# Handing the tokens of a hybrid block over channel by row, with the RMS norm factor applied as a row

## The chip, the cores and the metric

The kernel runs on one core of a Trainium2 chip. The metric is device microseconds of one execution, as the median of several runs. A core has a matrix engine (TensorE, PE in the profile, with its weight loads as PEld), a vector engine (VectorE, DVE), a scalar engine (ScalarE, ACT), GpSimd (POOL) and SyncE (SP), from whose queue most transfers (DMA) are issued. SBUF is the on-chip memory of 128 partitions; PSUM holds the results of TensorE in eight banks of 128 x 512 floats. Each engine takes its instructions in the order in which they were written and waits on semaphores for the others.

## What is computed

Two layers over 256 latent tokens `x` and 256 context tokens `ctx`, 2048 channels each. The change touches only the start of the first layer: the RMS norm of both token sets and their modulation.

```python
def rms_norm(x, g):
    y = xf * lax.rsqrt(jnp.mean(xf * xf, axis=-1, keepdims=True) + EPS)
    return (y * g.astype(jnp.float32)).astype(x.dtype)

def modulate(h, shift, scale):
    return h * (1 + scale) + shift
...
        shift, scale, gate = adaln(c, ada_w[i], ada_b[i])
        h = modulate(rms_norm(x, norm_g[i]), shift[:, None], scale[:, None])
        if needs_ctx:
            shift_c, scale_c, gate_c = adaln(c_ctx, ada_w[i], ada_b[i])
            hc = modulate(rms_norm(ctx, norm_g[i]), shift_c, scale_c)
...
    p = h @ w_in
    pc = hc @ w_in[:, base:]
```

`adaln` multiplies silu(c) by the modulation weights `ada_w` (2048 x 6144), whose first two thirds are the shift and the scale. After this the first layer runs neighbourhood attention and a state-space scan in parallel, and the second layer a gated short convolution. All data are float32.

## The kernel before

**Products.** An f32 product is made of three products in a faster form: both sides are split into a high part in that form (fp32r) and a low part, the rest. `hH[kb]` and `hL[kb]` are the high and low part of the modulated tokens for channel block kb (16 blocks of 128 channels), with the channels on partitions and 512 columns of tokens: latent tokens 0 to 255, then context tokens 256 to 511. Weight tiles arrive in `raw` buffers of 128 x 1024; ACT casts the high part (L420, or in halves L440) and DVE subtracts it for the low part (L427, L443), in one of three places `w`.

**Start.** The first part of the kernel goes in eight groups j of two channel blocks. For each group come the eight blocks of modulation weights (`ada`, four for the scale A0, four for the shift S0), multiplied with the conditioning vectors (L719), turned by TensorE and summed (L732 to L738). Then the modulated tokens of the group's two blocks are made (L757 to L763), and the group's part of the products is run: K and V for four token tiles t (0 and 1 latent, 2 and 3 context), Q for the latent tiles, and the first state-space columns (B) for all. K and V partial sums are copied out of PSUM in group 0 and added up on DVE afterwards (L787, L789). In group 0 the code writes the products of the latent tiles first (L875 to L889), then waits for the context tiles (L890).

**The tokens.** `x` and `cx` come as rows: 128 tokens on partitions, 2048 channels along. `x_norm` squares each row in four pieces with a running sum, on ACT (L601) and DVE (L603), makes the factor (mean, plus epsilon, power -0.5 on POOL, L571 and L572) and multiplies the row by it in place (L613, L615). `x_pair` then turns the row by TensorE, 128 x 128 at a time (`turn`, L199), two channel blocks to a bank, and ACT and DVE copy the bank into `xnT` (L628, L629). For group 0 the context tiles are handled one after the other, and the rest of their transposes come later. The context rows lie in the same places as the latent rows (`KT`, `KL`), so their loads wait until the latent rows have been turned.

**Order.** What is written out next is decided by a planner (`Plan`, L38) that keeps an estimated time for each engine and for the DMA. Tasks are generators: each names the engine and the operands that it needs next, and `pump` (L278) writes a step of the first task in the list `urgent` (then `side`, `back`) whose operands are estimated to be ready in time; `force` (L299) writes the earliest possible step until a condition holds. The list starts with the latent tokens, then the modulation task `ada_gen`, then the context tokens (L843 to L845). `ada_gen` is one task: it takes the groups one after another, and within a group first the modulation, then the scaled tokens. Loads are taken from a queue, `loads`, by `issue` (L365), in the order in which they were appended (L529 to L543); each needs a free `raw` buffer, of which there are nine at the start. Weights that are ahead get split by `split` and `low_part` (L405, L424); the latent step of group 0 writes the splits of V and Q itself, right behind its scaled tokens (L767 to L770).

## Time and profile before

| | us |
|---|---|
| Median of 3 runs | 1760.9 |
| Lowest and highest run | 1760.85, 1765.14 |
| Profiled execution, its own time | 1760.31 |
| Span of the profiled execution | 1758.5 |
| First modulation product | 10.82 |
| First K product of group 0 | 23.35 |
| First K product of group 1 | 54.30 |

A line of a group view names the source line, the engine, the operation, the tiles (out<-in), the shapes and the count, and then the busy time, the mean time of one in ns, and the idle time of the engine just ahead with what ended it. A line of the timeline begins with the start and the length in us. PE lines are listed by the helper that records them: L195 for all products, L199 for all transposes. For products in the form 128 x 512 the printed duration of one (about 390 ns) overlaps with the next; the distance between starts is what counts.

### The profile page before, as it was taken

What the parts mean: (1) busy time and instruction counts of PE and PEld (TensorE: products, weight loads), DVE (VectorE), ACT (ScalarE), POOL (GpSimd) and SP (SyncE); (2) the same over time, 40 slices, a digit from 0 to 9 for tenths busy, and PEclk for the clock granted to TensorE, in tenths of its full rate; (3) what the DMA queues carried; (4) which work ended last, traced back from release to release, by engine and by line L of the source; (5) the groups of instructions that cost most, each with busy time, mean ns of one, the idle gap of its engine ahead of it and who ended that gap; (6) DMA issues with size and microseconds to landing.
All of it is one profiled execution on the core that took longest, in us unless ns stands there. A gap on an engine that the chain in (4) does not pass through costs nothing.

```text
span 1758.5 us, 25025 instructions
## 1 busy us (share of the span) xinstructions
PE 1736.7 (99%) x9451; PEld 1463.1 (83%) x9451; DVE 1223.6 (70%) x1978; ACT 773.4 (44%) x1330; POOL 31.6 (2%) x28
## 2 busy tenths in 40 slices
PE   6999999999999999999999999999999999999998
PEld 4777988889888889888888898888888888888887
DVE  5666887878685878686877787787668555555554
ACT  5333544445242436343435343564446444444442
POOL 0000100001000000000000000000000000000000
PEclk9999999999999999999999999999999999999999
DMA  9987644686756767656776557768767666666563
GB/s 362 342 307 258 209 143 138 183 246 191 234 165 195 219 205 227 210 175 210 220 213 193 166 185 255 246 221 284 274 222 228 195 188 192 192 191 188 190 208 121
DMA packets 202536, 377.66 MB, mean 215 GB/s; under 512 B 32384, under 2 KB 69040, under 8 KB 202416
## 3 DMA queue, kind: packets, MB, share of 16 engines
q1 hardware_dynamic: 195152, 369.49, 65.5%
q10 hardware_dynamic: 7264, 6.58, 1.1%
q8 instruction: 74, 1.21, 0.3%
q14 instruction: 46, 0.38, 0.1%
HBM read 370.62 MB, written 6.71 MB: 215 GB/s over the span
## 4 chain that ended last, share of the span: by engine, by line
PE 94%; DMA 2%; DVE 2%; issue 1%; ACT 0%; POOL 0%; SPq 0%; ACTq 0%; DVEq 0%; POOLq 0%
PE bank L195 91%; PE bank L199 3%; DMA tmp<-dram_csr 1%; DVE w L427 1%; DMA raw<-in_ada 0%; DMA tmp<-dram_exr 0%; DMA raw<-in_adaT 0%; DVE tmp L1235 0%; ACT w L420 0%; POOL statk L572 0%; DVE mix L1562 0%; SPq L583 0%; DVE raw L823 0%; DVE tmp L603 0%; DVE Vt L1012 0%
## 5 line engine op out<-in xcount | busy, mean ns | idle before, releaser
L420 ACT CAST w<-raw 128x1024 fp32r<-128x1024 f32 x343 | 359.5, 1049 | 530.4 <-PE bank L195 447.7
L427 DVE TENSOR_TENSOR w<-raw,w 128x1024 fp32r<-128x1024 f32 x343 | 416.6, 1217 | 231.4 <-ACT w L420 230.1
L195 PE MATMUL bank<-hH,w 128*128 128x256 f32 (+1 forms) x2064 | 488.0, 324 | 1.2 <-DVE w L427 1.1
L195 PE MATMUL bank<-w,hH 128*128 128x512 f32 x1280 | 407.4, 396 | 2.7 <-ACT hH L757 2.5
L195 PEld LDWEIGHTS bank<-hH,w 128*128 128x128 f32 x2064 | 344.7, 188 | 34.2 <-DVE w L427 2.1
L195 PE MATMUL bank<-hL,w 128*128 128x256 f32 (+1 forms) x1040 | 334.3, 321 | 0.0
L195 PEld LDWEIGHTS bank<-w,hH 128*128 128x128 f32 x1280 | 237.7, 189 | 54.4 <-issue 4.0
L195 PE MATMUL bank<-w,hL 128*128 128x512 f32 x640 | 249.9, 391 | 0.1
L195 PEld LDWEIGHTS bank<-hL,w 128*128 128x128 f32 x1040 | 196.3, 189 | 14.9
L195 PE MATMUL bank<-w,h 128*128 128x512 f32 x768 | 179.7, 390 | 0.0
L823 DVE CUSTOM_DVE_ANT_0 raw<-raw,csb 128x1024 f32<-128x1024 f32 x128 | 155.4, 1219 | 26.2 <-DMA raw<-in_adaT 24.0
L195 PEld LDWEIGHTS bank<-w,h 128*128 128x128 f32 x768 | 143.6, 188 | 29.6
L195 PEld LDWEIGHTS bank<-w,hL 128*128 128x128 f32 x640 | 120.5, 188 | 25.4 <-DVE hL L763 0.6
L195 PE MATMUL bank<-w,mix 128*128 128x512 f32 x588 | 138.3, 391 | 0.9 <-DVE w L427 0.9
L195 PEld LDWEIGHTS bank<-w,mix 128*128 128x128 f32 x588 | 109.5, 188 | 24.0 <-DVE w L427 1.3
L1235 DVE SCALAR_TENSOR_TENSOR tmp<-bank,cwh,tmp 128x508 f32<-128x508 f32 (+1 forms) x96 | 71.0, 744 | 1.8
L195 PE MATMUL bank<-KL,h 128*128 128x512 f32 x264 | 63.8, 389 | 0.0
L427 DVE TENSOR_TENSOR KL<-raw,KL 128x1024 fp32r<-128x1024 f32 x32 | 39.1, 1223 | 33.1 <-ACT KL L420 33.1
L427 DVE TENSOR_TENSOR wL<-raw,wH 128x1024 fp32r<-128x1024 f32 x31 | 37.9, 1224 | 33.5 <-ACT wH L420 33.4
L427 DVE TENSOR_TENSOR QL<-raw,QT 128x1024 fp32r<-128x1024 f32 x32 | 39.2, 1224 | 29.8 <-ACT QT L420 29.8
L195 PEld LDWEIGHTS bank<-KL,h 128*128 128x128 f32 x264 | 49.5, 188 | 10.2
L195 PE MATMUL bank<-QT,h 128*128 128x512 f32 x168 | 56.2, 391 | 0.0
(291 smaller groups left out, 1984.7 us busy)
## 6 DMA issues: line engine op xcount, KB each, us to landing
raw<-in_w_in SPq DMA_DIRECT2D x196, 512.0 KB, 3.9
raw<-in_adaT SPq DMA_DIRECT2D x128, 512.0 KB, 4.8
raw<-in_sc_in SPq DMA_DIRECT2D x128, 512.0 KB, 3.8
raw<-in_w_out SPq DMA_DIRECT2D x64, 512.0 KB, 5.0
raw<-in_ada SPq DMA_DIRECT2D x34, 512.0 KB, 6.9
raw<-in_sc_out SPq DMA_DIRECT2D x32, 512.0 KB, 4.1
PT<-in_ada SPq DMA_DIRECT2D x16, 512.0 KB, 6.9
raw<-in_w SPq DMA_DIRECT2D x16, 512.0 KB, 6.1
```

The lines of the kernel that those rows point to most:

```text
L195: E(T.matmul(o, l, r, start=start, stop=stop, skip_group_check=True))
L199: E(T.transpose(o, i, ident if k == 128 else ident[:k, :k]))
L420: E(S.copy(H, v))
L427: E(V.tensor_tensor(out=Lo, in0=v, in1=H.bitcast(F32), op=ALU.subtract))
L823: E(V.tensor_tensor_reduce(out=raw, in0=raw, in1=csb, scale=1.0, scalar=0.0, op0=ALU.mult, op1=ALU.add, accum_out=gp[:, h, m:m + 1]))
L1235: E(V.scalar_tensor_tensor(out=do, in0=di, scalar=cwh[:, 32 * k + ch:32 * k + ch + 1], in1=do, op0=ALU.mult, op1=ALU.add))
```

## The change

The host hands both token sets over with channels on partitions: `xt` in two tiles of 8 channel blocks x 256 tokens, `ct` as one array of 16 blocks x 256 tokens. The row norm, its in-place scaling, the transposes and the copies (`x_norm`, `x_pair`) go. A new task `squares` squares the tokens two blocks at a time and sums over channels on TensorE: each 128 x 128 piece of the squares is the stationary side, and a column of ones is the moving side, so that the sum of each token lands on its own partition. For the latent tokens each of the eight pieces goes to TensorE (4 products each, the squares on ACT and DVE in turn); for the context ACT squares all eight, DVE adds the first seven up, and the sum and the last piece go to TensorE. The factor is made on 128 x 2 as before, broadcast along the free axis and turned by TensorE, so that `Rb` holds it as a row, the same on every partition. The scaled tokens are then made from the plain ones: DVE multiplies by A0 and by the row, ACT adds S0 for the high part, DVE adds S0 and subtracts the high part for the low one. In group 0 the two context tiles are now made together.

The context goes into places of its own (`QT`, `QL` and four of the `hL` tiles), and its load stands between the weights V and Q of group 0. The late halves of the small tables and of the constants are loaded after group 3 instead of before the second group's modulation weights. In group 0 the modulation products wait for one block each, not for two.

```diff
-    w_seg(0, CK, CV, CQ)
-    loads.append(lambda: x_load(2))
-    loads.append(lambda: x_load(3))
-    loads.append(lambda: E(DMA.dma_start(sm[:, NFIRST:], small[:, NFIRST:])))
-    loads.append(lambda: E(DMA.dma_start(cs_[:, CFIRST:], const[:, CFIRST:])))
+    w_seg(0, CK, CV)
+    loads.append(lambda: c_load())
+    w_seg(0, CQ)
...
+        if j == 3:
+            loads.append(lambda: E(DMA.dma_start(sm[:, NFIRST:], small[:, NFIRST:])))
+            loads.append(lambda: E(DMA.dma_start(cs_[:, CFIRST:], const[:, CFIRST:])))
...
+    one, Rb, *lplace = [st([128, 512], ("Bl", "Cl")[kb] if kb < 2 else f"hL{kb}", name=f"p{kb}") for kb in range(KB)]
+    E(V.memset(one, 1.0))
+    cplace += lplace[10:]
+    xT = [[xrow[k // 8][:, (k % 8) * 256:(k % 8) * 256 + 256], None] for k in range(KB)]
...
+    def squares(c):
+
+        yield when(lambda: xT[15][c] is not None)
+        acc, ps = None, None
+        for k in range(0, KB, 2):
+            src = xrow[k // 8][:, (k % 8) * 256:(k % 8) * 256 + 512]
+            if c:
+                src = cplace[k // 4][:, (k % 4) * 256:(k % 4) * 256 + 512] if k < 8 else cplace[k // 2 - 2]
+            onact = k % 4 == 0 or c == 1
+            yield W_("ACT" if onact else "DVE", src)
+            sq = tmp()
+            if onact:
+                E(S.activation(sq, src, AF.Square))
             else:
+                E(V.tensor_tensor(out=sq, in0=src, in1=src, op=ALU.mult))
+            if c and k < KB - 2:
+                if k == 0:
+                    acc = sq
+                    continue
+                yield W_("DVE", sq)
+                E(V.tensor_tensor(out=acc, in0=acc, in1=sq, op=ALU.add))
+                give(free_t, sq)
+                continue
+            parts = [acc, sq] if c else [sq]
+            for p in parts:
+                yield W_("PE", p, nb=0 if ps is not None else 1)
...
+                for h in range(2):
+                    for t in range(2):
+                        mm(ps[:, t:t + 1], p[:, h * 256 + t * 128:h * 256 + (t + 1) * 128], one[:, :1], f and not (h or t), True)
+                give(free_t, p)
+        r = rx[:, 2 * c:2 * c + 2]
+        yield W_("DVE", ps)
+        E(V.tensor_scalar(out=r, in0=ps[:, :2], scalar1=1.0 / D, scalar2=EPS, op0=ALU.mult, op1=ALU.add))
+        E(G.tensor_tensor(out=r, in0=r, in1=mhalf[:, :2], op=ALU.pow))
+        yield W_("PE", r)
+        for t in range(2):
+            turn(ps[:, 256 + t * 128:256 + (t + 1) * 128], r[:, t:t + 1].to_broadcast([128, 128]))
         yield W_("ACT", ps)
+        E(S.copy(Rb[:, c * 256:(c + 1) * 256], ps[:, 256:]))
         give(free_b, ps)
+        got.add(("r", c))
...
-                    w_ = 2 if j == 0 else 4
+                    w_ = 1 if j == 0 else 4
...
-            for ts in ((0, 1), (2,), (3,)) if j == 0 else ((0, 1, 2, 3),):
-                yield when(lambda: all(("xm", t, j) in got for t in ts))
+            for cs in ((0,), (1,)) if j == 0 else ((0, 1),):
+                yield when(lambda: all(("r", c) in got for c in cs))
...
-                        E(S.activation(hH[kb][:, ok_], xnT[kb][:, ok_], AF.Identity, scale=A0[:, kb, k:k + 1],
-                                       bias=S0[:, kb, k:k + 1]))
-                        E(V.tensor_scalar(out=hf[:, ok_], in0=xnT[kb][:, ok_], scalar1=A0[:, kb, k:k + 1],
-                                          scalar2=S0[:, kb, k:k + 1], op0=ALU.mult, op1=ALU.add))
+                    for c in cs:
+                        oc = slice(256 * c, 256 * c + 256)
+                        E(V.scalar_tensor_tensor(out=hf[:, oc], in0=xT[kb][c], scalar=A0[:, kb, c:c + 1], in1=Rb[:, oc],
+                                                 op0=ALU.mult, op1=ALU.mult))
+                        E(S.activation(hH[kb][:, oc], hf[:, oc], AF.Identity, scale=1.0, bias=S0[:, kb, c:c + 1]))
...
-                    E(V.tensor_tensor(out=hL[kb][:, o], in0=hf[:, o], in1=hH[kb][:, o].bitcast(F32), op=ALU.subtract))
+                    for c in cs:
+                        oc = slice(256 * c, 256 * c + 256)
+                        E(V.scalar_tensor_tensor(out=hL[kb][:, oc], in0=hf[:, oc], scalar=S0[:, kb, c:c + 1],
+                                                 in1=hH[kb][:, oc].bitcast(F32), op0=ALU.add, op1=ALU.subtract))
...
-    spawn(urgent, x_gen(0), 1)
+    spawn(urgent, squares(0), 1)
     spawn(urgent, ada_gen(), 2, 1)
-    spawn(urgent, x_gen(1), 1)
+    spawn(urgent, squares(1), 2)
```

More of the change, by code (lines that the diff above doesn't have):

```diff
@@ L141, with kernel @@
 @with_exitstack
-def kernel(ctx: ExitStack, tc, x, cx, ada0, w0, adaT, w_in, w_out, sc_in, sc_out, rpb, small, const,
+def kernel(ctx: ExitStack, tc, x, xt, ct, ada0, w0, adaT, w_in, w_out, sc_in, sc_out, rpb, small, const,
                        strict, rows, out):
@@ L617, in x_pair, with c_load @@
-    def x_pair(k2, ts):
-        yield W_("PE", *[XS[4 * t + k2 // 2] for t in ts], nb=1)
-        ps = bank()
-        n = 128 * len(ts)
-        for k in range(2):
-            kb = 2 * k2 + k
-            for i, t in enumerate(ts):
-                turn(ps[:, k * n + i * 128:k * n + (i + 1) * 128], XS[4 * t + kb // 4][:, (kb % 4) * 128:(kb % 4) * 128 + 128])
+    def c_load():
+        n = 0
+        for p in cplace:
+            m = p.shape[1] // 256
+            E(DMA.dma_start(p, ct[:, n * 256:(n + m) * 256]))
+            for k in range(m):
+                xT[n + k][1] = p[:, k * 256:(k + 1) * 256]
+            n += m
@@ L739, in ada_gen @@
                 give(free_b, ps)
-            for ts in ((0, 1), (2,), (3,)) if j == 0 else ((0, 1, 2, 3),):
-                yield when(lambda: all(("xm", t, j) in got for t in ts))
-                spans = [(k, slice(max(256 * k, 128 * ts[0]), min(256 * k + 256, 128 * ts[-1] + 128)))
-                         for k in range(2) if {2 * k, 2 * k + 1} & set(ts)]
-                o = slice(128 * ts[0], 128 * ts[-1] + 128)
+            for cs in ((0,), (1,)) if j == 0 else ((0, 1),):
+                yield when(lambda: all(("r", c) in got for c in cs))
+                o = slice(256 * cs[0], 256 * cs[-1] + 256)
                 for kb in (2 * j, 2 * j + 1):
@@ L1989 @@
     force(lambda: not urgent, (urgent,))
-_INS = ['x', 'cx', 'ada0', 'w0', 'adaT', 'w_in', 'w_out', 'sc_in', 'sc_out', 'rpb', 'small', 'const', 'strict', 'rows']
+_INS = ['x', 'xt', 'ct', 'ada0', 'w0', 'adaT', 'w_in', 'w_out', 'sc_in', 'sc_out', 'rpb', 'small', 'const', 'strict', 'rows']
 def kernel(**inputs):
```

73 lines of the change are left out of this document (20 added, 53 removed).

## The prediction, made before the changed kernel had run

> **What bounds the kernel now.** I read the page first, then the windows of the first 75 us, then the engine timelines inside them. Times are in us from the start of the span.
>
> ```profile
> PE 1736.7 (99%) x9451; PEld 1463.1 (83%) x9451; DVE 1223.6 (70%) x1978; ACT 773.4 (44%) x1330; POOL 31.6 (2%) x28
> ...
> PE   6999999999999999999999999999999999999998
> ```
>
> TensorE is busy 1736.7 of 1758.5 us; only the first of the 40 slices (44 us each) is far from full. All idle time of TensorE is 21.8 us. The change touches the head of the kernel and the scaled rows that feed it, so it can gain idle time of the head, or TensorE work that is in the way there, and nothing more.
>
> ```profile
> 0.00:13.00 13.00, 2.06 (x16) 0.43 (x16) 6.00 (x22) 6.38 (x14) 1.31 (x6) 1.00 0.83 310
> 13.00:17.50 4.50, 4.50 (x40) 4.28 (x40) 2.65 (x7) 3.04 (x9) 0.00 (x0) 1.00 1.02 411
> 17.50:23.35 5.85, 3.75 (x54) 1.67 (x46) 2.02 (x9) 2.22 (x6) 0.00 (x0) 1.00 1.04 412
> 23.35:33.40 10.05, 10.05 (x37) 7.81 (x38) 7.23 (x16) 7.55 (x14) 0.55 (x1) 0.83 1.03 400
> ...
> 54.30:75.50 21.20, 21.20 (x143) 16.10 (x143) 12.76 (x23) 6.31 (x10) 0.00 (x0) 1.00 0.95 347
> ```
>
> The columns are the stretch, its length, the busy time of PE, PEld, DVE, ACT and POOL, the granted clock, the DMA share and GB/s. Up to 23.35, when the first K product starts, the DMA is full and TensorE is not: this part waits for data. From 54.30 on TensorE has no gap at all, and VectorE is busy 60% of the time. What lies between is the ground of this change:
>
> ```profile
> 33.40:54.30 20.90, 19.15 (x170) 13.09 (x168) 14.40 (x39) 13.81 (x32) 1.06 (x3) 1.00 0.91 361
> 33.40:54.30 20.90, 4.74 (x36) 3.81 (x35) 1.00 0.91 361
> ```
>
> The first row is the whole stretch, the second the transposes (L199) in it. So 20.90 - 19.15 = 1.75 us are idle there, and a transpose costs 4.74 / 36 = 0.132 us of TensorE.
>
> **Part one: the latent tokens, up to the first product.** The 32 transposes of x between 13 and 17.5 go, with the copies of L628 and L629. In their place come 8 squares of 512 columns on ACT and DVE (the row norm needed as many) and 32 f32 products with one moving column. The kernel already has such products elsewhere:
>
> ```profile
> L195 PE MATMUL bank<-const,half 128*128 128x1 f32 x32 | 4.0, 229 | 0.0
> L199 PE MATMUL bank<-const,x 128*128 128x128 f32 x64 | 8.8, 290 | 0.3 <-ACT x L613 0.3
> L195 PE MATMUL bank<-PT,cpad 128*32 128x256 f32 x128 | 8.6, 381 | 0.0
> ```
>
> By the code those 32 instructions are 16 products (an f32 product shows as two instructions, as do the products with cpad: 8 for the 4 of one block). So one product is 2 x 4.0 / 32 = 0.25 us against 0.132 for a transpose, and 32 of them are 8.0 us where 4.2 stood. [...]
>
> These 8.0 us start when the first half row of x is squared, near 6, and end near 14.5. The modulation blocks wait behind them, and their four blocks of the scale part then run at once. What sets the end of this part is data, not TensorE:
>
> ```profile
> 9.42 0.33 SPq L381 DMA_DIRECT2D xtm<-in_ada  x1
> 10.71 0.33 SPq L381 DMA_DIRECT2D yi<-in_w  x1
> ...
> xtm<-in_ada SPq DMA_DIRECT2D x1, 512.0 KB, 10.2
> ...
> 20.57 0.61 PE L195 MATMUL bank<-xtm,cpad 128*32 128x256 f32 x8
> ...
> 22.44 0.16 DVE L738 TENSOR_TENSOR S<-S,small 128x4 f32<-128x4 f32 x1
> 22.64 0.41 DVE L759 TENSOR_SCALAR tmp<-xm,A,S 128x256 f32<-128x256 f32 x1
> ```
>
> The last modulation block lands at 9.42 + 10.2 = 19.6 and its products run at 20.57, behind the others. Taken block by block (the width 1 of the change) they can start at about 20.0, so the shift is ready some 0.5 us earlier. Against that, the scaled row now goes DVE, then ACT, then DVE, while before ACT read the normalised row beside DVE: 0.41 us more ahead of the first product. I take zero, with -0.4 to +0.7 as ends (the second block of channels waits once more for DVE).
>
> **Part two: the context tokens.** Their load is put between the weights V and Q. Before, V and Q came first and the context rows behind them:
>
> ```profile
> 17.37 1.77 SPq L583 DMA_DIRECT2D x<-in_cx  x4
> ...
> DMA to landing us min/median/max: 4.1/7.9/11.0
> ...
> 32.94 0.39 PE L195 MATMUL bank<-w,hL 128*128 128x512 f32 x1
> 33.17 0.39 PE L195 MATMUL bank<-w,hH 128*128 128x512 f32 x1
> 33.40 0.38 PE L199 MATMUL bank<-const,x 128*128 128x128 f32 x2
> 35.13 0.50 PE L195 MATMUL bank<-w,hH 128*128 128x512 f32 x1 [1.36 <-ACT hH L757]
> ```
>
> The last context load was issued about 18.7 and landed about 29.7 (11.0, the longest). The bytes ahead of Q in the new order are the same as those ahead of this load, so **Q lands near 29.7** and the context near 28.5. Q's split is queued on ACT and DVE before the context's squares: the split is written out right behind the first scaled row, and by the planner's own clock the context is not due by then. From here I step along, with these durations:
>
> ```profile
> L420 ACT CAST w<-raw 128x1024 fp32r<-128x1024 f32 x343 | 359.5, 1049 | 530.4 <-PE bank L195 447.7
> L427 DVE TENSOR_TENSOR w<-raw,w 128x1024 fp32r<-128x1024 f32 x343 | 416.6, 1217 | 231.4 <-ACT w L420 230.1
> L601 ACT ACTIVATE tmp<-x 128x512 f32<-128x512 f32 x8 | 5.0, 622 | 0.9 <-DMA x<-in_x 0.4 <-DMA x<-in_cx 0.4
> L789 DVE TENSOR_TENSOR sz<-sz,bank 128x512 f32<-128x512 f32 x2 | 1.4, 688 | 0.8 <-PE bank L195 0.7
> L572 POOL TENSOR_TENSOR rx<-rx,const 128x1 f32<-128x1 f32 x4 | 2.2, 552 | 35.4 <-DVE rx L571 35.4
> ```
>
> Cast to 30.7, low part to 31.9; the third product of Q needs it, and ten more at 0.23 (the starts 32.94 and 33.17 above) end at 34.2: **0.8 later** than the 33.4 of before. ACT squares all eight pieces of the context behind the cast, to 30.7 + 8 x 0.52 = 34.9 (0.62 each, 0.1 overlapped). DVE adds the first seven in six steps of about 0.62, 31.9 to 35.6. TensorE, in order, stands before the column sums from 34.2 to 35.6: **1.4 idle**. The sums are 8 products, 8 x 0.25 = **2.0**, with the last landing near 37.8; scaling, power on POOL (0.55) and their hand-overs take until 38.7: **1.0 idle**. Two transposes of the broadcast factor are **0.26**. ACT copies the row, DVE and ACT make the first scaled block by about 40.5; TensorE meanwhile runs the scale part of the next modulation block, 32 instructions at 8.6 / 128 = 0.067, 2.1 us. That cover rests on the order: it has landed (nothing but small loads was ahead of it) and the task issues it right behind the scaled rows. Without it another 1.4 us are idle.
>
> The removed side of the same stretch: 32 transposes, 4.2, and the 1.75 idle, which were the waits for each context tile in turn. Sum: -4.2 - 1.75 + 0.8 + 1.4 + 2.0 + 1.0 + 0.26 = **-0.5 us**.
>
> **Part three: the other seven groups.** Each block of 128 channels has on DVE 0.73 for two operations (L759) and 0.69 (L763 of 512 columns) before, and four two-input operations of 256 columns after:
>
> ```profile
> 46.47 0.73 DVE L759 TENSOR_SCALAR tmp<-xm,A,S 128x256 f32<-128x256 f32 x2
> 47.60 0.69 DVE L763 TENSOR_TENSOR hL<-tmp,hH 128x512 fp32r<-128x512 f32 x1 [0.39 <-ACT hH L757]
> ...
> 23.33 0.43 DVE L763 TENSOR_TENSOR hL<-tmp,hH 128x256 fp32r<-128x256 f32 x1 [0.28 <-ACT hH L757]
> ```
>
> 1.42 becomes 4 x 0.40 = 1.6 to 1.7, so 0.5 us more in a group of 21.2 us in which DVE is idle 8.4. Nothing here waits for it as long as the rows are made a group ahead; I take zero. The late half of the small tables moves behind group 3, 0.4 MB or 1 us of DMA out of the head, which TensorE does not wait for: zero. Where the rows stay longer in their places, the next writer is the first K norm after all eight groups: zero.
>
> The profiled execution took 1760.3 (span 1758.5 and 1.8 around it), 0.6 under the median of 1760.9. Forecast: 1760.3 - 0.5 = **1759.8**, no change that could be told. About 0.3%, 5.3 us, is what a measurement of this kernel can tell from none.
>
> **Rivals.** *A second slow stretch of the clock.* Now there is one:
>
> ```profile
> 24.00:25.00 1.00, 1.00 (x5) 0.60 (x4) 0.90 (x3) 1.00 (x2) 0.00 (x0) 0.82 0.98 393
> 25.00:26.00 1.00, 1.00 (x4) 0.81 (x3) 1.00 (x3) 1.00 (x2) 0.00 (x0) 0.50 1.05 418
> ...
> 28.00:29.00 1.00, 1.00 (x6) 0.83 (x5) 1.00 (x4) 0.92 (x2) 0.00 (x0) 0.97 1.05 384
> ```
>
> It follows the thin stretch from 17.5 to 23.35 (TensorE busy 3.75 of 5.85), lasts about 3.4 us at 0.50 and so costs 1.7. The new wait from 34.2 to 38.7 holds only 2 us of one-column products. If that brings a second slow stretch, the time is 1759.8 + 1.7 = 1761.5. For it: the wait is as thin. Against: from 33.40 to 35.13 TensorE did next to nothing and the clock stayed at 1.00. Chance 0.25. [...]
>
> *The waits do not come.* If the context is squared before Q's split, the sums lie behind V's products and neither wait shows: 1.4 + 1.0 + 0.8 come off, 1756.6; if the slow stretch then falls where TensorE waits for data, 1.7 more, 1754.9. For it: the context lands before Q. Against: ACT and DVE keep their order, and Q's split was queued first. Chance 0.15, half of it under 1755.6; a start at the early end of its bound adds 0.03.
>
> *Slower: the longer chain in the groups.* Each block now goes DVE, ACT, DVE on 256 columns, and hH waits for the first DVE step. DVE also releases the product banks (the additions of L789, 0.69 each). Where it stands in order before ACT while a bank waits, TensorE loses the step ahead of ACT, 0.43, and the 0.28 by which DVE's four operations are longer: 0.7 a block, in 14 blocks 9.9 us, 1759.8 + 9.9 = 1769.7. It decides from the point at which only one bank is free when a block's rows are made; at half of the blocks it gives 1764.8. Against it: TensorE has no gap from 54.30 to 75.50 with the like waits now. Chance 0.15, two thirds of it over 5.3 us; waits of the head wider than my bounds add 0.03.
>
> *The change gives less than it says.* The transposes go, but the column sums put 80 instructions (10 us by the row) where 64 (8.8) were. That is inside the forecast.
>
> **How the numbers follow.** Forecast 0.45, slow clock 0.25, no waits 0.15, chain 0.15. The ends: price of the 16 instructions from 0.066 to 0.23 each, -1.0 to +1.7; the missing cover, +1.4; the start, -0.4 to +0.7. Range 1755.0 to 1765.5. Faster by over 0.3%: 0.11; slower: 0.13; the rest, 0.76, is within.
>
> **What would show it.** Right: the products with one moving column at 0.125 an instruction; Q's products ending 33.5 to 34.5; the column sums of the context starting 1 to 2 us later on DVE's add; the same point of the weights' order (first K product of group 1) within 1.5 us of 54.3, allowing for 1.9 us of the modulation of group 2 that stood ahead of it; no gap of TensorE afterwards. Wrong: the context's squares ahead of Q's cast on ACT; a clock of 0.50 again near 38 to 42; idle time of TensorE after 54 that names the scaled rows or the bank additions.

## The result and the profile after

| | before | after |
|---|---|---|
| Median of 7 runs each, side by side (us) | 1763.17 | 1773.84 |
| Lowest and highest | 1760.85, 1768.93 | 1770.47, 1778.70 |
| Ratio, 95% interval | | 1.0061 [1.0041, 1.0081] |
| Profiled execution, its own time | 1760.31 | 1778.70 |
| First K product of group 0 | 23.35 | 30.77 |
| First B product of group 0 (the group's last part) | 49.37 | 55.83 |
| First B product of group 1 | 70.60 | 79.75 |
| First B product of group 7 | 192.41 | 202.08 |

The change made the kernel slower by 10.7 us; forecast were 1759.8 and a range up to 1765.5. The profiled execution of the changed kernel is the slowest of its seven, 4.9 above their median, so below I count at milestones inside the head: at the first B product of group 7, the last of the groups, it stands at +9.67, which is nearly the whole difference of the medians. Source lines of the changed kernel are numbered on their own (L196 the products, L200 the transposes).

The first row is from the page of the changed kernel (busy time of the engines), the others are from its windows, cut at the milestones:

```profile
PE 1750.4 (99%) x9471; PEld 1472.7 (83%) x9471; DVE 1218.5 (69%) x1952; ACT 761.7 (43%) x1301; POOL 31.7 (2%) x26
```

```profile
13.00:17.50 4.50, 4.50 (x23) 4.50 (x22) 0.00 (x0) 0.00 (x0) 0.00 (x0) 1.00 1.02 411
17.50:30.77 13.27, 10.89 (x87) 5.95 (x86) 1.41 (x8) 2.20 (x6) 0.70 (x1) 1.00 0.82 274
30.77:40.40 9.63, 9.37 (x36) 6.21 (x36) 8.47 (x13) 8.53 (x16) 0.00 (x0) 1.00 1.01 402
40.40:44.00 3.60, 2.12 (x18) 2.02 (x18) 0.75 (x3) 0.41 (x1) 0.92 (x3) 0.99 0.83 330
44.00:55.83 11.83, 11.83 (x94) 7.28 (x94) 4.13 (x12) 4.09 (x9) 0.29 (x2) 0.86 0.70 236
55.83:79.75 23.92, 21.27 (x141) 15.58 (x140) 14.36 (x28) 8.48 (x15) 0.00 (x0) 1.00 0.92 337
```

The kernel before, from its first K product to the first B products of groups 0 and 1:

```profile
23.35:49.37 26.02, 24.27 (x161) 17.97 (x161) 17.42 (x50) 18.00 (x42) 1.61 (x4) 0.93 0.94 365
49.37:70.60 21.23, 21.23 (x141) 15.51 (x140) 13.87 (x25) 7.65 (x14) 0.00 (x0) 1.00 1.00 381
```

**The loss has two places.** Up to the first K product the change loses 30.77 - 23.35 = 7.42. From there to the first B product it wins: 9.63 + 3.60 + 11.83 = 25.06 against 26.02, -0.96. In group 1 it loses again, 23.92 against 21.23, +2.69: TensorE, which had no gap there, is idle 2.65. The six groups after that add 122.33 - 121.81 = 0.52. Together 9.67. "Busy" does not mean fast: from 13 to 17.5 TensorE is busy all the time with 23 instructions, where the kernel before ran 40.

**The first place, on TensorE's timeline of the changed kernel:**

```profile
6.71 13.79 PE L196 MATMUL bank<-p,tmp 128*128 128x1 f32 x64 [6.71 <-DVE p L586]
20.43 1.08 PE L196 MATMUL bank<-raw,cpad 128*32 128x256 f32 x8
...
22.15 2.79 PE L196 MATMUL bank<-raw,cpad 128*32 128x256 f32 x24
...
27.75 0.60 PE L196 MATMUL bank<-xtm,cpad 128*32 128x256 f32 x8
...
30.77 0.50 PE L196 MATMUL bank<-w,hH 128*128 128x512 f32 x1 [1.36 <-ACT hH L760]
```

The 64 one-column instructions take 13.79 / 64 = 0.215 each, not 0.125, and end at 20.5, not 14.5. Behind them the modulation products also crawl: 2.79 / 24 = 0.116 each, against 8.6 / 128 = 0.067 in the row of the prediction. Both are slower by about 1.7, and the timeline puts no wait for a transfer between them. The last modulation products then start at 27.75; before, it was 20.57. From there to the first K product it is 3.02 against 2.78. So the late sums and the slow modulation behind them are 7.18 of the 7.42.

The late modulation also holds back the loads, since V needs a buffer that a modulation block has to leave. SP's queue of the kernel before, then SP's queue and two windows of the changed kernel:

```profile
12.06 1.59 SPq L381 DMA_DIRECT2D raw<-in_w  x2
```

```profile
21.57 0.33 SPq L382 DMA_DIRECT2D raw<-in_w  x1
```

```profile
20.00:21.00 1.00, 1.00 (x11) 0.61 (x10) 0.16 (x1) 0.00 (x0) 0.22 (x1) 1.00 0.16 62
21.00:22.00 1.00, 0.97 (x10) 0.29 (x2) 0.00 (x0) 0.00 (x0) 0.48 (x1) 1.00 0.00 0
```

V is issued at 21.57 instead of 12.06, and the DMA runs empty, at 62 and 0 GB/s.

**The second place** is the second block of group 1. The timeline of the changed kernel, ACT, DVE and TensorE:

```profile
56.85 2.00 ACT L421 CAST w<-raw 128x1024 fp32r<-128x1024 f32 x2
...
57.31 0.48 DVE L758 SCALAR_TENSOR_TENSOR tmp<-c,A,p 128x256 f32<-128x256 f32 x1
...
58.76 0.57 ACT L790 COPY Vt<-bank 128x512 f32<-128x512 f32 x1
...
59.23 0.91 ACT L760 ACTIVATE hH<-tmp,S 128x256 fp32r<-128x256 f32 x2
...
59.77 0.88 DVE L765 SCALAR_TENSOR_TENSOR hL<-tmp,S,hH 128x256 fp32r<-128x256 f32 x2 [1.98 <-ACT hH L760]
60.57 2.35 DVE L428 TENSOR_TENSOR w<-raw,w 128x1024 fp32r<-128x1024 f32 x2
...
61.84 0.49 PE L196 MATMUL bank<-w,hH 128*128 128x512 f32 x1 [2.65 <-DVE w L428]
```

DVE has its first step ready at 57.8. The second one, on ACT, stands behind two casts and a copy and starts at 59.23. DVE's third step, hL, waits 1.98 for it, and behind hL in DVE's order stand the low parts of the weights, which TensorE needs next: 2.65 idle.

### The profile page after: what moved, and what is told of

The parts are those of the page before. It is cut to its first block, busy times and chain, and to the rows that moved or that the text cites. A ratio compares the mean times of both kernels' runs of the same rounds, so it can differ in the third digit from the quotient of the medians.

```text
span 1776.9 us, 24977 instructions
## 1 busy us (share of the span) xinstructions
PE 1750.4 (99%) x9471; PEld 1472.7 (83%) x9471; DVE 1218.5 (69%) x1952; ACT 761.7 (43%) x1301; POOL 31.7 (2%) x26
## 4 chain that ended last, share of the span: by engine, by line
PE 93%; DVE 3%; DMA 2%; ACT 1%; issue 1%; POOL 0%; SPq 0%; ACTq 0%; DVEq 0%; POOLq 0%
PE bank L196 90%; PE bank L200 3%; DVE w L428 1%; DMA tmp<-dram_csr 1%; DMA raw<-in_w_in 1%; ACT w L421 0%; DVE tmp L1239 0%; DMA bias<-dram_rpbs 0%; DMA small<-in_small 0%; DVE tmp L620 0%; POOL statk L574 0%; DVE raw L826 0%; DVE mix L1566 0%; ACT tmp L1404 0%; SPq L1043 0%
## 5 line engine op out<-in xcount | busy, mean ns | idle before, releaser
L196 PE MATMUL bank<-hH,w 128*128 128x256 f32 (+1 forms) x2064 | 488.0, 324 | 4.4 <-DVE w L428 4.4
L196 PE MATMUL bank<-w,hH 128*128 128x512 f32 x1280 | 408.2, 396 | 4.5 <-DVE w L428 2.7
L196 PEld LDWEIGHTS bank<-hH,w 128*128 128x128 f32 x2064 | 344.9, 188 | 37.5 <-DVE w L428 5.6
L196 PE MATMUL bank<-hL,w 128*128 128x256 f32 (+1 forms) x1040 | 334.3, 322 | 0.0
L196 PEld LDWEIGHTS bank<-w,hH 128*128 128x128 f32 x1280 | 236.7, 188 | 59.0 <-issue 4.9
L196 PE MATMUL bank<-w,hL 128*128 128x512 f32 x640 | 249.5, 390 | 0.0
L196 PEld LDWEIGHTS bank<-hL,w 128*128 128x128 f32 x1040 | 196.3, 189 | 14.9
L196 PE MATMUL bank<-w,h 128*128 128x512 f32 x768 | 179.7, 390 | 0.1
L196 PEld LDWEIGHTS bank<-w,h 128*128 128x128 f32 x768 | 143.6, 188 | 29.9 <-ACT h L1707 0.3
L196 PE MATMUL bank<-w,mix 128*128 128x512 f32 x588 | 139.8, 394 | 3.6 <-ACT w L421 2.1
L196 PEld LDWEIGHTS bank<-w,hL 128*128 128x128 f32 x640 | 120.1, 188 | 24.8 <-DVE hL L765 0.4
L196 PEld LDWEIGHTS bank<-w,mix 128*128 128x128 f32 x588 | 110.7, 190 | 27.5 <-ACT w L421 2.6
L196 PE MATMUL bank<-KL,h 128*128 128x512 f32 x264 | 63.8, 389 | 0.0
L196 PEld LDWEIGHTS bank<-KL,h 128*128 128x128 f32 x264 | 49.5, 188 | 10.2
L196 PE MATMUL bank<-QT,h 128*128 128x512 f32 x168 | 56.1, 391 | 0.0
```

The source lines that it names most:

```text
L196: E(T.matmul(o, l, r, start=start, stop=stop, skip_group_check=True))
```

## The experiments

Each is the changed kernel with one edit, unless it says "on the kernel before". Ratios are to the kernel before, in the same batch. K, B0 and B7 are the first K product and the first B products of groups 0 and 7, in the profiled execution. The planner writes the order anew for every edit, so an experiment can move more than its lines say; that is told where the trace shows it.

K, B0 and B7 stand on one profile each, and they move by themselves. The trace keeps a record of the clock granted to TensorE, and the time of its first entry, a 1.00, differs between equal starts: the change, e4 and e6 have the same instructions of TensorE up to K, the first entry at 26.86, 25.67 and 30.36, and K at 30.77, 30.30 and 32.35. e5, e9, e10, e11 and e13 have one start in common, the first entry at 15.38 to 17.38, and K at 22.77 to 23.73. So differences of 1 to 2 us at a milestone are not told from none here.

| | median | before | ratio [95%] | K | B0 | B7 |
|---|---|---|---|---|---|---|
| before | | | 1 | 23.35 | 49.37 | 192.41 |
| the change | 1773.84 | 1763.17 | 1.0061 [1.0041, 1.0081] | 30.77 | 55.83 | 202.08 |
| e1_preadd | 1771.74 | 1763.11 | 1.0050 [1.0031, 1.0068] | 24.72 | 51.73 | 199.56 |
| e2_warm | 1773.45 | 1763.11 | 1.0058 [1.0037, 1.0080] | 29.03 | 53.36 | 199.85 |
| e3_wide | 1768.38 | 1763.11 | 1.0028 [1.0015, 1.0041] | 24.38 | 51.18 | 197.46 |
| e4_order | 1780.39 | 1763.11 | 1.0099 [1.0078, 1.0120] | 30.30 | 59.61 | 209.44 |
| e5_prewide | 1769.31 | 1765.50 | 1.0025 [1.0012, 1.0038] | 22.77 | 51.19 | 198.10 |
| e6_pair | 1773.74 | 1765.50 | 1.0051 [1.0038, 1.0065] | 32.35 | 58.43 | 205.97 |
| e7_widepair | 1772.07 | 1765.50 | 1.0046 [1.0028, 1.0063] | 25.19 | 52.73 | 201.36 |
| e8_all | 1771.89 | 1765.50 | 1.0038 [1.0023, 1.0054] | 22.64 | 51.21 | 200.23 |
| e9_nocsum | 1768.92 | 1764.58 | 1.0022 [1.0008, 1.0036] | 23.16 | 44.19 | 199.07 |
| e10_nogate | 1774.66 | 1764.58 | 1.0055 [1.0034, 1.0075] | 22.77 | 51.17 | 202.59 |
| e11_lateq | 1772.99 | 1764.58 | 1.0046 [1.0027, 1.0065] | 23.73 | 51.97 | 203.54 |
| e12_chain (on before) | 1767.45 | 1764.58 | 1.0020 [1.0005, 1.0035] | 24.38 | 50.96 | 194.00 |
| e13_apart | 1768.33 | 1763.61 | 1.0034 [1.0019, 1.0048] | 23.23 | 53.13 | 199.41 |
| e14_apartearly | 1768.82 | 1763.61 | 1.0038 [1.0023, 1.0053] | 22.26 | 54.09 | 200.42 |
| e15_headload (on before) | 1769.68 | 1763.61 | 1.0039 [1.0024, 1.0054] | 33.02 | 57.79 | 200.71 |

None beat the kernel before.

### Is it the head's one-column sums, and why are they slow?

**e1_preadd**: the latent squares are all made on ACT and added on DVE, as the context's are, so that 16 instead of 64 instructions are left.

```diff
-            if c and k < KB - 2:
+            if k < KB - 2:
...
-            parts = [acc, sq] if c else [sq]
+            parts = [acc, sq]
```

> The changed kernel, with the latent squares summed like the context's: ACT squares all eight pieces, DVE adds the first seven, so that 8 column-sum products (16 instructions) stand in the head instead of 32 (64). The instructions of TensorE otherwise keep their order. Theory (the head: 64 one-column instructions at 0.215 us in front of the modulation products): the column sums end near 14.5 instead of 20.4, the first K product starts at 23.0 to 24.5 instead of 30.77, and the time falls by 6 to 7.5, to 1766 to 1768. Rival (the loss lies behind the head, in the context's wait, the second slow stretch and the chain of the groups): the first K product moves up, but the time falls by less than 3, since the next wait takes it back.

**e2_warm**: five products of zeros, not used for anything, ahead of everything.

```diff
+    for i in range(NWARM):
+        mm(wps, zero[:, :128], zero, True, True)
```

> The changed kernel with 5 f32 products of 128x512 on a tile of zeros ahead of everything, into a bank that is not used for them otherwise. Theory A (the one-column instructions cost 0.215 us because the clock of TensorE is still at half, which the granted clock does not show before its first change): they cost about 0.125 in the head too, end near 15.5, first K product near 26, time lower by 4 to 5.5, at 1768 to 1770. Theory B (0.215 is their price on these operands, whatever the clock): they end near 20.5 as before and the time stays at 1773 to 1775.

**e3_wide**: all sums, the 64 instructions of the head and the 16 of the context, against 128 columns of ones instead of one.

```diff
-                        mm(ps[:, t:t + 1], p[:, h * 256 + t * 128:h * 256 + (t + 1) * 128], one[:, :1], f and not (h or t), True)
+                        mm(ps[:, t * 128:(t + 1) * 128], p[:, h * 256 + t * 128:h * 256 + (t + 1) * 128], one[:, :128], f and not (h or t), True)
```

> The changed kernel with a moving side of 128 columns of ones instead of one column, in all column sums (40 products), so that each gives 128 equal columns. Theory A (work in the array wakes the clock, and one column is too little work): the 64 instructions of the head begin at 0.21 or more and fall to about 0.13 after 3 to 4 us, end at 16 to 18, first K product 26 to 28, time lower by 2 to 4. Theory B (price by the instruction, not by the clock): 64 instructions at 0.215 or more to the end, end at 20.5 or later, time the same or higher by up to 3.

TensorE's timeline in the wide version:

```profile
6.70 9.58 PE L196 MATMUL bank<-p,tmp 128*128 128x128 f32 x64 [6.70 <-DVE p L586]
...
17.68 1.50 PE L196 MATMUL bank<-raw,cpad 128*32 128x256 f32 x24
...
24.38 0.74 PE L196 MATMUL bank<-w,hH 128*128 128x512 f32 x2 [1.36 <-ACT hH L760]
```

With 128 times the work per instruction the sums take 9.58 instead of 13.79, 0.150 each, and the modulation products behind them 1.50 / 24 = 0.063 instead of 0.116. By their starts in the trace, the wide instructions come every 0.213 us up to 11.3 and every 0.112 behind it; the 64 of the changed kernel come every 0.213 to the end. So up to 11.3 both widths cost the same. A single column is not slow by its data here: with it TensorE stayed at the rate of 0.213, and the modulation products behind it at 0.116. e2 shows the reverse, timeline and windows:

```profile
8.34 9.10 PE L197 MATMUL bank<-p,tmp 128*128 128x1 f32 x64
```

```profile
6.00:13.00 7.00, 7.00 (x49) 5.64 (x47) 3.37 (x9) 2.00 (x4) 0.00 (x0) 1.00 1.01 402
13.00:14.00 1.00, 1.00 (x8) 1.00 (x7) 0.00 (x0) 0.00 (x0) 0.00 (x0) 0.66 1.04 422
14.00:15.00 1.00, 1.00 (x7) 1.00 (x6) 0.00 (x0) 0.00 (x0) 0.00 (x0) 0.50 1.04 418
```

Warmed up first, the same instructions go at 9.10 / 64 = 0.142 on the mean, and in the middle of them, with TensorE busy 1.00, the granted clock falls to 0.50. By their starts they come every 0.112 us up to this drop, at 13.3, and every 0.213 behind it: 0.213 is the price at the granted clock of 0.50, and 0.112, at 1.00, is what the wide ones cost behind 11.3. One-column products did not hold the clock here: it fell 5.0 us behind the start of the first, at 8.34.

The column of the clock reads 1.00 all through the slow head of the changed kernel, but it does so because nothing is recorded there. The first entry of the clock record, a 1.00, is at 26.86 in the changed kernel, at 11.32 in e3 and at 6.50 in e2, and at each of these times the instructions of TensorE change from the slow rate to the fast one (in the changed kernel the modulation products, four at a time, from one start in 0.427 us to one in 0.216). That the clock is at half ahead of the first entry is read from these rates, of which the slow one, 0.213, is that of e2 at a granted 0.50.

e1 brings K back to 24.72, 6.05 earlier, but B7 only 2.52, and its interval overlaps the change's: its theory held at K, its rival for the time. Its 16 instructions still take 3.57 (0.223 each), and later in the groups its clock is granted at 0.50 twice, 5.13 us lost (the time at 0.50, counted half) against 1.71 in the kernel before. e2 gains only 1.74 at K: the clock falls again before the modulation. e3 has theory A's course: in the middle of the sums the rate goes from one in 0.213 us to one in 0.112.

**e5_prewide**: e1 and e3 together.

> The changed kernel with the latent squares summed on DVE first (8 products) and all column sums with a moving side of 128 columns. Theory (two terms in the head: the number of the column sums, and the clock that one column does not keep awake): first K product at 23.5 to 24.5, no second slow stretch near 38 to 44 as with one column, time 1765 to 1768, below both single edits (1771.7 and 1768.4) or at the lower of them. Rival (the clock falls for want of any work of TensorE, whatever the width of the sums): with less work in the head the clock is still at half when the modulation starts, a second slow stretch stays, and the time is 1769 to 1772.

K is at 22.77, 0.58 ahead of before: the head's loss is undone. At B7 the kernel is still 5.69 behind, and its time is no better than e3's. From K to B7 TensorE is idle 6.57 us in it against 1.97 before, from K to B0 alone 4.21 against 1.75. TensorE's waits in it:

```profile
31.13 0.50 PE L196 MATMUL bank<-w,hH 128*128 128x512 f32 x1 [1.42 <-ACT w L421]
32.39 1.20 PE L196 MATMUL bank<-w,hH 128*128 128x512 f32 x2 [0.53 <-DVE w L428]
...
40.06 0.43 PE L200 MATMUL bank<-const,rx 128*128 128x128 f32 x2 [1.04 <-POOL rx L636]
...
52.60 0.73 PE L196 MATMUL bank<-hH,w 128*128 128x512 f32 x2 [0.80 <-DVE w L428]
...
56.61 0.51 PE L196 MATMUL bank<-w,hH 128*128 128x512 f32 x1 [0.74 <-ACT hH L760]
```

Those at 31.13 and 32.39 name Q's split, which had time in the changed kernel because TensorE came 8 us later: the late head had covered them.

**e15_headload**, on the kernel before: 32 one-column products (64 instructions) of the squares that it makes anyway, results not used.

```diff
+            if t < 2:
+                yield W_("PE", jk, nb=0 if extra else 1)
...
+                for i in range(4):
+                    mm(extra[0][:, i:i + 1], jk[:, i * 128:(i + 1) * 128], ident[:, :1], True, True)
```

> The kernel before, with 32 f32 products of one moving column (64 instructions) on the squared pieces of the latent tokens, as the change has them, ahead of the modulation, their results not used. Theory (the head alone): they take 0.2 us or more each and end near 20, the transposes come behind them, the first K product starts at 30 to 33, and the time is 5 to 9 above the kernel before. Rival (a late head is caught up by waits that it covers): the first K product is late, but the time is less than 4 above.

```profile
6.85 13.78 PE L195 MATMUL bank<-const,tmp 128*128 128x1 f32 x64 [6.85 <-DMA const<-in_const]
20.57 1.93 PE L195 MATMUL bank<-raw,cpad 128*32 128x256 f32 x16
22.43 4.64 PE L199 MATMUL bank<-const,x 128*128 128x128 f32 x32
27.00 1.07 PE L195 MATMUL bank<-raw,cpad 128*32 128x256 f32 x16
...
33.02 0.73 PE L195 MATMUL bank<-w,hH 128*128 128x512 f32 x2 [1.11 <-ACT hH L766]
```

Nothing else of the change is in this kernel, and the 64 instructions take the same 13.78. The modulation instructions take 1.93 / 16 = 0.121 behind them and 1.07 / 16 = 0.067 once the 32 transposes have run; the first entry of the clock record is at 24.37, in the middle of the transposes. So the one-column products alone cost +8.30 at B7 and 0.39% of the time. It keeps the transposes, which the change does not have, so its head is not the change's own: +9.67 at K against the change's +7.42.

### The other terms

**e4_order**: the context load again behind Q.

```diff
-    w_seg(0, CK, CV)
+    w_seg(0, CK, CV, CQ)
     loads.append(lambda: c_load())
-    w_seg(0, CQ)
```

> The changed kernel with the context's load behind the weights K, V and Q of group 0, as before the change, instead of between V and Q. Theory (the head): the first K product stays at 30.8 and the time within 2 of 1773.8, since Q is not what TensorE waits for. Rival (the order of the loads costs, because Q's split stands ahead of the context's squares): Q's products end 1 us or more earlier, and the time falls by 1 to 3.

B0 comes 3.78 later than in the change and the time is the worst of all, which neither the theory nor the rival had. The place of the load was a gain, not a cost.

**e9_nocsum**: on e5, the context takes the latent factor, so its squares, sums and waits are left out.

```diff
+        if c:
...
+            E(S.copy(Rb[:, 256:], Rb[:, :256]))
```

> As e5_prewide, but the context's squares, sums and factor are left out: the context takes the factor of the latent tokens. Its load and its place in the order stay. Theory (what is left after the head is the wait for the context's factor, some 6 us between Q's products and the context's in which TensorE runs only the sums and the next modulation block): the context's first product moves from about 42.5 to 36 to 37, and the time falls by 4 to 6 against e5_prewide, to 1763 to 1765.5. Rival (what is left is the chain DVE, ACT, DVE in the groups and the order that follows from it): the first B product moves up but is given back by the waits of groups 1 to 7, and the time falls by less than 2.

B0 is at 44.19, 7.0 earlier than in e5, but B7 is at 199.07 against 198.10. The whole gain is given back in group 1, which takes 31.42 against 23.41 in e5. Most of that is one wait, for the scaled tokens of group 1, whose modulation is not done yet, and the clock at 0.50 behind it, from 53.7 to 60.5, which loses 3.4:

```profile
53.70 0.80 PE L196 MATMUL bank<-w,hH 128*128 128x512 f32 x1 [3.83 <-ACT hH L766]
```

**e12_chain**, on the kernel before: ACT makes the high part out of DVE's row instead of beside it.

```diff
-                        E(S.activation(hH[kb][:, ok_], xnT[kb][:, ok_], AF.Identity, scale=A0[:, kb, k:k + 1],
-                                       bias=S0[:, kb, k:k + 1]))
...
+                        E(S.copy(hH[kb][:, ok_], hf[:, ok_]))
```

> The kernel before, with one thing of the change: the high part of the scaled tokens is taken by ACT from DVE's product (DVE, then ACT, then DVE) instead of by ACT from the normalised tokens beside DVE. Theory (the longer chain alone costs): first K product 0.4 later and one or two gaps in groups 1 and 2, together 1 to 3, so 1764.5 to 1766.5. Rival (the chain costs only together with the late modulation of group 1): within 1 of the kernel before.

Its transposes, the timeline around its first K product, and its next wait:

```profile
12.96 5.27 PE L199 MATMUL bank<-const,x 128*128 128x128 f32 x32
18.16 1.07 PE L195 MATMUL bank<-raw,cpad 128*32 128x256 f32 x16
...
23.27 0.16 DVE L738 TENSOR_TENSOR S<-S,small 128x4 f32<-128x4 f32 x1
...
24.38 0.73 PE L195 MATMUL bank<-w,hH 128*128 128x512 f32 x2 [1.31 <-ACT hH L759]
35.79 0.50 PE L195 MATMUL bank<-w,hH 128*128 128x512 f32 x1 [1.88 <-ACT hH L759]
```

From the shift to the first K product it is 24.38 - 23.27 = 1.11, before 23.35 - 22.44 = 0.91: the chain itself costs 0.20 there. The other 0.83 of the +1.03 at K is not the chain. The same 32 transposes take 5.27 instead of 4.36, so that the modulation behind them starts at 18.16, not at 17.32: the clock's first entry is at 16.20 here and at 14.40 in the kernel before, with the same instructions of TensorE up to there. At the context tokens the same wait is 1.88 instead of 1.36. At B7 it is +1.59, about half of which can be that later clock, and the time over 12 runs is 0.20% [0.05, 0.35] longer.

### Attempts on the waits that are left

**e6_pair**, on the change: both blocks of a group are made in one step, so that no split comes in between. **e7_widepair**: that with e3. **e8_all**: e5 and e6, with the product of A0 and the factor taken early in group 0.

```diff
-                    if j:
+                    if j and kb % 2 == 0:
...
-                    yield W_("DVE", Rb[:, o])
+                    if not j or kb % 2 == 0:
+                        yield W_("DVE", Rb[:, o])
```

> The changed kernel in which the two channel blocks of a group are written out together (from group 1 on), so that on ACT no weight cast stands between the high parts of the two. Theory (the chain DVE, ACT, DVE puts the late high part of the second block ahead of the low part of the weights K of group 1 on DVE): the 2.65 us gap of TensorE near 59 goes, and the time falls by 2 to 3, to 1771 to 1772. Rival (the gap is DVE's load or the arrival of the weights): it stays, and the time stays at 1773 to 1775.

> The changed kernel with 128 columns on the moving side of the column sums (all 40 products) and the blocks of a group in pairs. Theory: the two are separate terms, but the gap of the pair was smaller with the wide sums (waits of 0.4 to 0.8 in group 1), so the pair adds 0.5 to 1.5 to the gain of the wide sums: 1766.5 to 1768. Rival (one term hides the other): 1768.4 as with wide sums alone.

> Wide column sums, squares summed first, pairs, and in group 0 the latent product with scale and factor made as soon as the scale is there, ahead of the shift. Theory (what is left in the head is the longer chain from the shift to the first product): first K product at 23.0 to 23.8, time 1762 to 1765, so no worse than 0.1% above the kernel before and perhaps level with it. Rival (what is left is the wait for the context's factor and its slow stretch): first K product moves up but the time stays at 1765 to 1768.

In e6 the 2.65 is gone. In its place stand waits of 1.15 on a cast of ACT and 0.52 on its low part in the same group, and a second slow stretch of the clock (5.11 lost in the two): from B0 to the first B product of group 1 it is 24.79 against 23.92. Its interval overlaps the change's. e7 and e8 are not better than e3 and e5, which lack this edit.

**e10_nogate**, on e5: the rows of the next group no longer wait until DVE is nearly as early as TensorE in the plan.

```diff
-                        yield when(lambda: need[0] >= j or plan.t["DVE"] <= plan.t["PE"] + 600)
+                        pass
```

> As e5_prewide, without the condition that holds a group's scaled tokens back until DVE is estimated to be free or the group is needed. Theory (groups are made too late for the longer chain): the waits of 0.7 to 0.8 in group 1 shrink and the time falls by 1 to 3, to 1766 to 1768. Rival (the modulation of the group itself is late, since its task stood behind the context): no change of the waits in group 1, time 1768 to 1771.

**e11_lateq**, on e5: Q's split is written after the context's squares.

```diff
-                    split()
...
-            w3 = [use(k) for k in range(3)]
+            w3 = [use(k) for k in range(2)]
...
+            w3.append(use(2))
```

> As e5_prewide, with Q's split written out where Q is used, behind the context's squares, instead of right behind the latent scaled tokens. Theory (the context's squares stand behind Q's cast on ACT and Q's low part on DVE): the context's sums start at 34 to 35 instead of 37, its first product 2 to 3 earlier, the time falls by 1 to 3, to 1766 to 1768. Rival (Q's products are then late by as much, since its cast and low part come behind 4 us of squares): the sums wait in order behind Q's products, no gain, 1768.5 to 1771.

Both are later than e5 at B7, by 4.49 and 5.44; e11 loses 6.83 us to the slow clock in its profile.

**e13_apart**, on e5: the context tokens of group 0 become a task of their own, so that the modulation of group 1, now taken block by block, can run in their waits. **e14_apartearly**: that, with A0 times the factor taken early.

```diff
-            for cs in ((0,), (1,)) if j == 0 else ((0, 1),):
...
+            yield from tokens(j, (0,) if j == 0 else (0, 1))
+            if j == 0:
+                urgent.insert(0, Task(tokens(0, (1,)), 1, 0))
```

> As e5_prewide, with the context's scaled tokens of group 0 in a task of their own, so that the modulation of group 1 no longer stands behind the context's factor in the modulation task, and its products are taken block by block. Theory (behind the head, the loss is TensorE waiting for the context while the modulation of group 1, which has landed, is not allowed ahead, and group 1 then starting late): the 64 modulation instructions of group 1 lie in the waits near 31 to 40, first B product at 46.5 to 48.5 instead of 51.19, no gap over 0.5 in group 1, the time falls by 2 to 4 against e5_prewide, to level with the kernel before or 0.1% above. Rival (the loss is DVE and ACT, which are behind by then): the first B product moves up by less than 1.5 or is given back in group 1, ratio 1.002 or more.

> As e13_apart, and the latent product with scale and factor of group 0 made ahead of the shift, so that the chain to the first product is no longer than in the kernel before. Theory (the longer chain costs 0.4 to 1 at the first product, as in e12_chain): first K product 0.3 to 0.8 earlier than in e13_apart, time lower by 0.5 to 1.5. Rival (TensorE then waits for Q's weights instead): no difference from e13_apart.

B0 comes 1.94 and 2.90 later than in e5, B7 1.31 and 2.32 later. In e13 the waits for the context's factor and scaled tokens are down to 0.54 and 0.74, those for Q's split stay (1.29 and 0.52), and a new one of 1.68 on the low part comes at 55.54. In e14 the early product shortens the wait ahead of the first K product from 1.36 to 0.97, but the time does not follow.

## Why the prediction was wrong

**Part one failed, at its price and so at its end.** "One product is 2 x 4.0 / 32 = 0.25 us", "end near 14.5", "What sets the end of this part is data, not TensorE", "I take zero". The step that failed is the price of the head's sums, 0.125 an instruction, and with it that TensorE would be done before the data. 0.125 is the price of 32 instructions between 402 and 1194 us, where TensorE had been at work and the clock was granted at 1.00; 16 of them later in the changed kernel do take 1.95 / 16 = 0.122. In the head it is 0.215, and the sums end at 20.5. Then TensorE sets the end, and its slow modulation products come on top. e15 shows the cost alone: 0.39% [0.24, 0.54], against 0.61% [0.41, 0.81] for the change; e3, which only widens the moving side, takes 4.62 of the 9.67 at B7 away.

Two things in my own text should have led there. I gave the price "0.066 to 0.23 each" as ends, but used them for the 16 instructions of the context alone; on the 64 of the head the upper end is 14.7 us, ending at 21. And the kernel before had two rows of the same form on its timeline, the first one ahead of the transposes that I took away:

```profile
10.82 2.28 PE L195 MATMUL bank<-raw,cpad 128*32 128x256 f32 x16 [10.82 <-DMA raw<-in_ada]
13.03 4.36 PE L199 MATMUL bank<-const,x 128*128 128x128 f32 x32
17.32 1.07 PE L195 MATMUL bank<-raw,cpad 128*32 128x256 f32 x16
```

16 instructions in 2.28, and in 1.07 once the transposes had run. The transposes were not only work in the way: while they ran, TensorE came to its faster rate, by their starts from one in 0.213 us to one in 0.109, at 14.4, and the modulation products went from 0.14 to 0.067. The granted clock of 1.00 beside them hid that. e15 has the same step across them, 0.121 to 0.067, and in e12 TensorE had run hardly anything but transposes from 12.96 on when its clock came up at 16.20. That it was the transposes that brought the clock up is my reading of these rows; no run shows them alone.

**The start** was put at "-0.4 to +0.7", with 0.41 more for the longer chain. DVE's timeline of the changed kernel, the last step of the shift:

```profile
29.61 0.16 DVE L740 TENSOR_TENSOR S<-S,small 128x4 f32<-128x4 f32 x1
```

From there to the first K product the change has 30.77 - 29.61 = 1.16 against 0.91, +0.25. That was within the bounds and is not where the time went.

**Part two was about right.** Its sum was -0.5; the stretch from K to B0 has -0.96. The steps, shifted by the late head, on the timeline and the windows of the changed kernel:

```profile
40.86 1.95 PE L196 MATMUL bank<-p,tmp 128*128 128x1 f32 x16 [0.45 <-DVE tmp L620]
43.84 0.64 PE L200 MATMUL bank<-const,rx 128*128 128x128 f32 x2 [1.04 <-POOL rx L636]
```

```profile
44.00:45.00 1.00, 1.00 (x10) 0.44 (x13) 0.08 (x1) 0.37 (x1) 0.29 (x2) 0.50 0.00 0
45.00:46.00 1.00, 1.00 (x16) 0.43 (x12) 0.42 (x2) 0.51 (x1) 0.00 (x0) 0.50 0.11 24
```

The sums take 1.95 (forecast 2.0), the wait for the factor is 1.04 (1.0), the one for DVE's adds 0.45 (1.4, since Q's products came later than the adds expected), and Q's 0.8 did not show. The rival of the slow clock came true in its place, 0.50 right behind these waits, but instead of the earlier stretch and not beside it: 1.71 us are lost to it by the record in both kernels.

**Part three failed.** "I take zero" stands against +2.69 in group 1 and +0.52 after it. The operation was mis-sized a little (0.48 instead of 0.40 for one of 256 columns). What failed is the reason, that nothing waits as long as the rows are made a group ahead: they are not in group 1, which comes straight behind the late context. The third rival had the mechanism, DVE standing in order behind ACT's step, but put it at the banks and at 0.7 a block over 14 blocks. It showed once, at the weights' low part, as 2.65.

**How the parts add up.** The head alone (e15) has +8.30 at B7 and the chain alone (e12) +1.59, together 9.89; the change has 9.67. In the times it is 0.39 + 0.20 = 0.59% against 0.61%. This fits, but is no proof of a sum: e15 keeps the transposes, and up to half of e12's 1.59 is the later clock of its profile. Taking the head's cost away inside the change (e5) brings the time from 0.61% to 0.25%, 0.36, about what e15 adds. By the one profile of each it gives less, 3.98 at B7: e5 is ahead of before at K and 5.69 behind at B7. What the kernel loses then lies mostly in the waits shown for e5, on splits, factor and tokens. Each attempt to move one of them (e6 to e8, e10, e11, e13, e14) brought another. Which share of these 5.69 is the chain and which is that the transposes no longer fill the waits stays open.

**After the head** the profiled executions differ by 8.7 us more. TensorE's waits around the first products with w_out, before and after:

```profile
1122.46 6.90 PE L195 MATMUL bank<-w,mix 128*128 128x512 f32 x29 [0.91 <-DVE w L427]
```

```profile
1137.39 0.49 PE L196 MATMUL bank<-w,mix 128*128 128x512 f32 x1 [2.14 <-ACT w L421]
1139.38 8.47 PE L196 MATMUL bank<-w,mix 128*128 128x512 f32 x29 [1.50 <-DVE w L428]
```

Behind these waits the changed kernel's clock falls to 0.50 once more, from 1139.6 to 1143.0. e13 has no such wait there, with the same code behind the head; e12, on the kernel before, has 2.59 and 1.50; and the medians differ by hardly more than B7 does. So I do not count this to the change. What brings these waits in some profiles and not in others stays open.

## What to carry to other kernels

Price an operation by a row from the same surroundings: what TensorE did in the microseconds before changed its rate by 1.9 here (0.213 against 0.112), and work that is removed may have been what made it fast. When a sum is turned over to TensorE as products with one moving column near a start or a wait, try the moving side at 128 columns as well; here that was the cheaper form, 9.58 us against 13.79 for the 64 of the head. A bound that you put on a price belongs to every place where the price is used. And compare milestones of single profiles only above what they move by themselves, here up to 2 us.

## What was unexpected

A stationary side of 128 x 128 f32 against one column took 0.215 an instruction in the head and 0.122 later, against 128 columns 0.150 in the head, the head's each over 64 instructions: there, the wider form was the faster, since the clock came up in the middle of it. With TensorE busy 1.00 on one-column products the granted clock fell to 0.50, at 13.3 (e2). The granted clock read 1.00 in a stretch in which two kinds of products ran at little more than half their later rate (0.215 and 0.116 an instruction, later 0.122 and 0.065). And the time at which the clock came up differed by up to 4.7 us (25.67 and 30.36) behind the same instructions of TensorE.
